# Moving the opening's sums of squares and modulation tiles between engines

## The chip, the cores and the metric

The kernel runs on one core of a Trainium2 chip. The metric is device time in microseconds (us), the median of several executions. The engines of a core work from queues of their own: TensorE (PE, with its weight loads shown apart as PEld), VectorE (DVE), ScalarE (ACT), GpSimd (POOL), and SyncE (SP), which here issues nearly all DMA transfers.

## The reference

One inference step of a one-layer hybrid trunk, over 512 prompt tokens and 32 sample tokens at once (544 columns), with 1024 features. What matters here is the beginning:

```
mod = silu(c) @ w_ada + b_ada        # shift1, scale1, gate1, shift2, scale2, gate2
h   = rms_norm(x, g_norm1) * (1 + scale1) + shift1
q, k, v, B, C, u, g_a, g_b = split(h @ w_in)
```

`c` has two rows, one of the prompt and one of the sample, so each of the six modulations is 1024 features by 2. Behind it come stick-breaking attention of 16 heads, a short gated convolution, two branch products, an output product, a second norm and a convolutional FFN, all of which the change leaves alone.

## The kernel before, in words

Activations lie feature by token: 8 feature tiles of 128 partitions, 544 columns each, in two halves of 272. A product in nearly full precision is made of three products of rounded parts: each operand is split in a high part `h` and a low part `l` (ACT casts the high part, DVE or POOL subtracts for the low one), and TensorE sums high by high, high by low and low by high. One output tile is a loop over the 8 feature tiles of the input, called a step each, with 3 x 2 = 6 matmuls of 272 columns in a step (`mm3_steps`, L112), 48 in a product.

The opening, up to the first attention scores, is this:

- Eight transfers bring `xt`, one brings `c` to all partitions (`cbc`). ACT squares each tile (L289), DVE adds the squares (`sacc1`, L291), and two fp32 matmuls with a matrix of ones (L294) give the sums over features in every partition. `rstd_of` makes the inverse root `y1` of them: Ln and Exp on ACT (L171, L173), four operations on DVE (L172 to L177).
- `mod(s, k, on_pe)` makes one of the 16 tiles of scale1 and shift1: a transfer of 512 KB into one of seven buffers `mraw` (L305), then one of two ways. On DVE, `dot` (L197) multiplies the tile by each row of silu(c) and sums, two passes over 1024 columns. On TensorE (L309) silu(c) (`sct`, 128 x 2) is the stationary operand and the tile of weights the moving one, eight fp32 matmuls of 128 columns; an fp32 matmul stands in the trace as two records, so a tile has 16. The 2 x 128 result is copied by ACT (`rc`, L312) and transposed by TensorE (L314). ACT then adds the bias and writes `mods` (L319, L321).
- Ten tiles go to DVE (all scale1, and shift1 of k = 5 and 6), six to TensorE.
- For each k, `xt` is multiplied by `y1` (L331, on POOL for four of the eight, on DVE for the others), ACT applies scale and shift (L333), and the result is split in `hh` and `hl` (L91 and L92).
- Four weight tiles of `w_in` are loaded and split meanwhile (`load_w`, L99 on ACT and L100 on POOL): for queries 0, keys 0, values 0 and queries 1.
- In program order the products of queries 0 and keys 0 (in the PSUM tiles called `slot`) come after all that, then `fill(13)`: the eight steps of values 0 and five of queries 1. `queries` and `keys` (L233 to L248) turn the results into operands for the scores `z` (L362). The `slot` tiles must be read before `z` may take their PSUM.

The order is not that of the source: a planner goes through the program and puts each engine's instructions in a fixed order by priority (earlier in the program first) and by when its own cost model thinks that their inputs are there. On the chip each engine then works strictly in this order and waits where an input is late. [...]

Of the kernel before, what the change touches and what calls it, by code (L numbers as in the profile page):

```python
# [12 lines left out]
F32 = mybir.dt.float32  # L13
F32R = mybir.dt.float32r
AF = mybir.ActivationFunctionType
ALU = mybir.AluOpType
# [18 lines left out]
# Token columns of every [feature, token] tile, as two halves, the latest token first:  # L35
# prompt 511..256 | sample 31..16, prompt 255..0 | sample 15..0.
# [4 lines left out]
# Columns of the per-partition vectors that are packed into one array.  # L41
# [9 lines left out]
def build(tc, a):  # L51
    nc = tc.nc
    ctx = ExitStack()
    with ctx:
# [4 lines left out]
        # ---------------------------------------------------------------- constants  # L59
# [16 lines left out]
        # ---------------------------------------------------------------- helpers  # L76
        def two(t):
            """A [p, T] view as its two halves."""
            return t.rearrange("p (a c) -> p a c", a=2)

        def parts(t):
            """Prompt columns and sample columns of a [p, 2, HT] view."""
            return t[:, :, 0:HP], t[:, :, HP:HT]

        def inorder(t):
            """Prompt and sample columns, as halves, of a [p, T] view with all prompt columns first."""
            return two(t[:, 0:SEQ]), two(t[:, SEQ:T])

        def split(hi, lo, x, eng=nc.vector):
            """hi + lo == x, each with 12 significant bits."""  # L90
            nc.scalar.copy(hi, x)  # L91
            eng.tensor_tensor(lo, x, hi.bitcast(F32), ALU.subtract)  # L92
# [32 lines left out]
        def proj(w, x):  # L125
            """Product with a weight tile, in DRAM or loaded."""
            if not isinstance(w, tuple):
                w = load_w(w)
            ps = acc()
            mm3(ps, *w, *x)  # L130
            return ps

        def steps(src, post, lo):
            """The product of x with a weight tile in steps, and what follows it."""
            w = src if isinstance(src, tuple) else load_w(src, lo=lo)
            ps = acc()
            yield from mm3_steps(ps, *w, *x)
            post(ps)
# [6 lines left out]
        def fill(n):  # L145
            """n steps of the products that wait in the queue."""
            while n and queue:
                try:
                    next(queue[0])
                    n -= 1  # L150
                except StopIteration:
                    queue.popleft()

        def after(inst, earlier):
            """Order two instructions of one engine."""
            tc.add_manual_dep(inst.ins, earlier.ins.name,
                              mybir.DependencyInfo(mybir.DependencyClass.NoSync, mybir.DependencyReason.DATA))

        def log_tables(earlier):
            """Load the table set that has Ln and Exp, after an activation that needs another one."""  # L160
            t = nc.scalar.add_instruction(mybir.InstLoadActFuncSet(
                name=nc.get_next_instruction_name(), act_func_set_id=6, engine=mybir.EngineType.Activation,
                ins=[], outs=[]))
            after(t, earlier)
            return t

        def rstd_of(pool, ss_ps, y, tables):
            """y = (mean + eps) ** -0.5 of the column sums in psum, in every partition."""
# [5 lines left out]
            # one Newton step: y * (1.5 - 0.5 v y y)  # L174
# [9 lines left out]
        # ---------------------------------------------------------------- adaLN  # L184
# [9 lines left out]
        def dot(raw, sums):  # L194
            """Each row of raw times silu(c), summed."""
# [4 lines left out]
        def ada(s, t):  # L200
            """mods[:, s, t, :]: one feature tile of one of the last four modulations, both batches."""
# [9 lines left out]
        # ---------------------------------------------------------------- first norm, first projections  # L211
# [6 lines left out]
        def flat(ps, name):  # L218
            """psum to [p, T] with all prompt columns first."""
# [9 lines left out]
        def queries(j, ps):  # L229
            """A head's (hi, lo) over each other, hi on the head's own partitions."""  # L230
# [7 lines left out]
        def keys(j, ps):  # L238
            """A head's (hi, hi) and (lo, lo)."""
# [16 lines left out]
        def values_t(j):  # L256
            """[keys, quarters]: head 0 hi, lo; head 1 lo, hi."""
# [11 lines left out]
        # sample queries, keys and values of all heads, kept until all are there  # L269
# [14 lines left out]
        nc.sync.dma_start(cbc, a["c"].rearrange("(o n) d -> o n d", o=1).broadcast_to([P, 2, D]))  # L284
        silu = nc.scalar.activation(cbc, cbc, AF.Silu)
        sacc1 = stp.tile([P, T], F32, name="sacc1")
        for k in range(KD):
            sq = sacc1 if k == 0 else stp.tile([P, T], F32, tag="sq", bufs=3, name="sq")
            nc.scalar.activation(sq, xt[:, k], AF.Square)  # L289
            if k:  # L290
                nc.vector.tensor_tensor(sacc1, sacc1, sq, ALU.add)  # L291
        ss = slots[0][:, :, 0:HT]
        for i in range(2):
            nc.tensor.matmul(ss[:, i], ones, two(sacc1)[:, i], start=True, stop=True)  # L294
# [7 lines left out]
        def mod(s, k, on_pe):  # L302
            """mods[:, s, k, :]: one feature tile of one of the first two modulations."""
            raw = stp.tile([P, D], F32, tag="araw", bufs=7, name="mraw")
            nc.sync.dma_start(raw, a["w_shift"][k] if on_pe else a["w_ada"][s * KD + k])  # L305
            if on_pe:
                rows = mt[0:2, 0, k % 4 * P:k % 4 * P + P]
                for i in range(KD):
                    nc.tensor.matmul(rows, sct[:, i], raw[:, i * P:i * P + P], start=i == 0, stop=i == KD - 1,  # L309
                                     skip_group_check=True)  # L310
                rc = stp.tile([2, P], F32, tag="rc", bufs=2, name="rc")
                nc.scalar.copy(rc, rows)  # L312
                sums = mt[:, 1, 2 * k:2 * k + 2]
                nc.tensor.transpose(sums, rc, ident[0:2, 0:2])  # L314
# [8 lines left out]
        ws = []  # L323
        for k in range(KD):
            if k in (1, 2, 4, 5):
                src = (W[0], W[KD], W[2 * KD], W[1])[len(ws)]
                ws.append(load_w(src, pool=stp if len(ws) < 2 else wp, lo=nc.gpsimd))
            mod(1, k, False)
            mod(0, k, k not in (5, 6))
            hf = xt[:, k]  # L330
            (nc.gpsimd if k in (1, 2, 4, 6) else nc.vector).tensor_tensor(hf, hf, y1, ALU.mult)  # L331
            for n, v in enumerate(parts(two(hf))):
                nc.scalar.activation(v, v, AF.Identity, scale=mods[:, 1, k, n:n + 1], bias=mods[:, 0, k, n:n + 1])  # L333
            split(hh[:, k], hl[:, k], hf, nc.gpsimd if k in (4, 5) else nc.vector)
        for w, slot, post in zip(ws, slots, (queries, keys)):
            ps = slot[:, :, 0:HT]
            mm3(ps, *w, *x)
            post(0, ps)
        task(values, 0, ws[2])
        task(queries, 1, ws[3])  # L340
        fill(13)
# [3 lines left out]
        # ---------------------------------------------------------------- projections and prompt attention  # L345
# [18 lines left out]
        def causal(t, width, fill):  # L364
            """Fill where the key is not before the query: [queries, blocks of width keys], last key first."""
# [4 lines left out]
        def scores(j, e):  # L370
            """One head's weights for the prompt: queries on partitions, keys from the last one back."""
# [27 lines left out]
        def transposed(sg):  # L399
            """The weights with keys on partitions, split, by rows of key blocks."""  # L400
# [15 lines left out]
        def weighted(j, e, rows, vt):  # L416
            """Weights times values, into the pair's features."""
# [17 lines left out]
        # ---------------------------------------------------------------- short conv: B * dwconv(C * u)  # L435
        def padded(t):
            """Prompt and sample columns, as halves, of a row of two stretches with two pads after each."""
# [10 lines left out]
        def conv(c, u, w, b, i):  # L448
            """Three causal taps over u's two padded stretches, latest token first."""
# [63 lines left out]
        # ---------------------------------------------------------------- sample attention, half of the heads  # L513
        def sample_steps(p0):
            """Heads of the pairs p0..p0+3: four heads' queries on the partitions, two such groups."""
# [55 lines left out]
            # the shares of the weights' high and low parts, then of the values' high and low parts  # L571
# [33 lines left out]
        # ---------------------------------------------------------------- branches and merge  # L605
# [32 lines left out]
        # ---------------------------------------------------------------- out projection, residual, second norm  # L638
# [8 lines left out]
        def streams(c0, c1):  # L647
            """The stretches of prompt and of sample columns in c0..c1, of one half."""
# [3 lines left out]
        def residual(ps, s, m, c0, c1):  # L652
            """xr[m] += gate * psum in the columns c0..c1; its squares into sacc, the last ones into sq2."""
# [11 lines left out]
        def norm(c0, c1, tables, parts_):  # L665
            """The rstd of the columns c0..c1."""
# [8 lines left out]
        def h2(c0, c1, earlier=None):  # L675
            """The second norm's output in the columns c0..c1."""
# [45 lines left out]
        # ---------------------------------------------------------------- conv FFN  # L722
# [30 lines left out]
        # the last tile's weights stay, so that one half's norm runs beside the other half's product  # L753
# [88 lines left out]
```

## Time and profile before

| | us |
|---|---|
| median of 3 runs | 1123.7 (1121.96 to 1124.98) |
| profiled execution, first to last instruction (span) | 1122.7 |
| profiled execution, whole time | not listed; the span stands 1.0 below the median |
| PE busy | 1053.6 (94%) |
| PEld busy | 1027.6 (92%) |
| DVE busy | 666.1 (59%) |
| ACT busy | 428.6 (38%) |
| POOL busy | 262.4 (23%) |
| first score matmul `z` starts | 72.78 |

Busy times are unions over an engine's instructions. The end of a matmul in the records is modelled, so spacings between starts say more than durations. [...] A stretch before the first recorded change of the clock is shown as 1.00.

### The profile page before, as it was taken

How to read it: one execution, taken by the hardware profiler on the slowest of the kernel's cores; microseconds unless marked ns; L12 is line 12 of the kernel's file. 1: busy time of each engine (PE TensorE's matmuls, PEld its weight loads, DVE VectorE, ACT ScalarE, POOL GpSimd, SP SyncE). 2: the span in 40 equal slices, each digit the busy share in tenths (PEclk: the TensorE clock that was granted, in tenths of full speed). 3: DMA queues.
4: the chain of work that ended last, by engine and by line, in shares of the span. 5: the costliest groups of instructions: out<-in, count | busy, mean ns of one | idle time of the engine just before them, and what ended most of it. 6: DMA issues, size and time to landing. Idle time of an engine off the chain costs nothing.

```text
span 1122.7 us, 19599 instructions
## 1 busy us (share of the span) xinstructions
PE 1053.6 (94%) x8042; PEld 1027.6 (92%) x8042; DVE 666.1 (59%) x1005; ACT 428.6 (38%) x749; POOL 262.4 (23%) x384
## 2 busy tenths in 40 slices
PE   3898888898999999999999999899999999999995
PEld 1688787887999999999999999899999999999995
DVE  6967787776775534666677756755455455422334
ACT  5466566565643322222222253333333333322230
POOL 3434455443321101211211215300010010001112
PEclk9899999999999999999999999899999999999998
DMA  9612121211122222455455463022222222222212
GB/s 372 217 40 95 58 78 50 73 61 67 68 88 73 79 73 94 152 187 175 165 182 178 167 228 115 1 74 78 95 91 79 95 93 77 87 90 85 85 53 80
DMA packets 38153, 120.60 MB, mean 107 GB/s; under 512 B 4272, under 2 KB 7472, under 8 KB 37936
## 3 DMA queue, kind: packets, MB, share of 16 engines
q1 hardware_dynamic: 37920, 119.22, 30.9%
q8 instruction: 63, 1.03, 0.4%
q10 hardware_dynamic: 144, 0.14, 0.1%
q14 instruction: 26, 0.21, 0.1%
HBM read 112.60 MB, written 6.75 MB: 106 GB/s over the span
## 4 chain that ended last, share of the span: by engine, by line
PE 79%; DVE 10%; ACT 4%; issue 3%; POOL 2%; DMA 1%; DVEq 0%; SPq 0%; ACTq 0%; POOLq 0%
PE ps L112 72%; DVE keep L392 3%; PE o L362 2%; PE at L408 1%; POOL keep L367 1%; DVE hf L682 1%; DVE sg L393 1%; ACT keep L388 1%; DVE adum L197 1%; PE slot L112 1%; DVE kt L246 1%; DMA cbc<-in_c_dram 1%; ACT wh L99 1%; PE so L362 1%; ACT sg L389 1%
## 5 line engine op out<-in xcount | busy, mean ns | idle before, releaser
L99 ACT CAST wh<-raw 128x1024 fp32r<-128x1024 f32 x153 | 159.7, 1045 | 349.0 <-PE ps L112 246.0
L100 DVE TENSOR_TENSOR wl<-raw,wh 128x1024 fp32r<-128x1024 f32 (+1 forms) x120 | 146.4, 1222 | 169.6 <-ACT wh L99 169.0
L112 PE MATMUL ps<-hh,wh 128*128 128x272 f32 x992 | 212.0, 295 | 8.1 <-ACT qs L235 8.1
L112 PE MATMUL ps<-hl,wh 128*128 128x272 f32 x992 | 206.8, 290 | 0.0
L112 PE MATMUL ps<-hh,wl 128*128 128x272 f32 x992 | 206.6, 290 | 0.0
L112 PEld LDWEIGHTS ps<-hh,wh 128*128 128x128 f32 x992 | 157.9, 191 | 11.0 <-ACT qs L235 9.6
L112 PEld LDWEIGHTS ps<-hl,wh 128*128 128x128 f32 x992 | 157.8, 191 | 0.0
L112 PEld LDWEIGHTS ps<-hh,wl 128*128 128x128 f32 x992 | 156.9, 191 | 0.0
L112 PE MATMUL ps<-h2l,wh 128*128 128x272 f32 x704 | 150.6, 290 | 0.9 <-DVE h2l L92 0.9
L112 PE MATMUL ps<-h2h,wh 128*128 128x272 f32 x704 | 150.9, 290 | 0.3 <-ACT h2h L91 0.3
L112 PE MATMUL ps<-h2h,wl 128*128 128x272 f32 x704 | 151.1, 291 | 0.0
L100 POOL TENSOR_TENSOR wl<-raw,wh 128x1024 fp32r<-128x1024 f32 x33 | 81.9, 2481 | 203.9 <-ACT wh L99 194.3
L112 PEld LDWEIGHTS ps<-h2l,wh 128*128 128x128 f32 x704 | 113.4, 190 | 1.7 <-DVE h2l L92 1.7
L112 PEld LDWEIGHTS ps<-h2h,wh 128*128 128x128 f32 x704 | 113.6, 190 | 0.9 <-ACT h2h L91 0.8
L112 PEld LDWEIGHTS ps<-h2h,wl 128*128 128x128 f32 x704 | 112.6, 190 | 0.0
L197 DVE SCALAR_TENSOR_TENSOR adum<-araw,cbc 128x1024 f32<-128x1024 f32 x64 | 82.7, 1293 | 41.8 <-DMA araw<-in_w_ada_dram 41.0
L392 DVE TENSOR_TENSOR_SCAN keep<-keep,zero 128x512 f32<-128x512 f32 (+1 forms) x64 | 65.9, 1041 | 8.1 <-POOL keep L367 6.3
L112 PE MATMUL ps<-fl,wh 128*128 128x272 f32 x308 | 63.9, 288 | 0.0
L367 POOL TENSOR_SCALAR_AFFINE_SELECT keep<-keep 128x128 f32<-128x128 f32 x64 | 44.3, 693 | 83.5 <-issue 43.7
L112 PE MATMUL ps<-fh,wh 128*128 128x272 f32 x308 | 63.6, 288 | 0.0
L112 PE MATMUL ps<-fh,wl 128*128 128x272 f32 x308 | 63.5, 288 | 0.0
L662 POOL TENSOR_TENSOR sacc<-sacc,sq 128x272 f32<-128x272 f32 x24 | 27.5, 1162 | 143.3 <-ACT sq L660 143.3
(200 smaller groups left out, 1745.6 us busy)
## 6 DMA issues: line engine op xcount, KB each, us to landing
raw<-in_w_in_dram SPq DMA_DIRECT2D x64, 512.0 KB, 3.3
raw<-in_w_up_dram SPq DMA_DIRECT2D x44, 512.0 KB, 3.3
araw<-in_w_ada_dram SPq DMA_DIRECT2D x32, 512.0 KB, 4.0
raw<-in_w_down_dram SPq DMA_DIRECT2D x16, 512.0 KB, 3.5
mraw<-in_w_ada_dram SPq DMA_DIRECT2D x10, 512.0 KB, 7.3
raw<-in_w_branch_b_dram SPq DMA_DIRECT2D x8, 512.0 KB, 3.2
raw<-in_w_branch_a_dram SPq DMA_DIRECT2D x8, 512.0 KB, 3.3
raw<-in_w_out_dram SPq DMA_DIRECT2D x8, 512.0 KB, 3.8
```

The source lines that it names most:

```text
L99: nc.scalar.copy(wh[:, :nk], raw[:, :nk])
L100: lo.tensor_tensor(wl[:, :nk], raw[:, :nk], wh[:, :nk].bitcast(F32), ALU.subtract)
L112: nc.tensor.matmul(ps[:, i, 0:c1 - c0], w[:, k], x[:, k0 + k, c0:c1], start=s, stop=e)
L197: nc.vector.scalar_tensor_tensor(adum, raw, 1.0, cbc[:, n], ALU.mult, ALU.mult, accum_out=sums[:, n:n + 1])
L246: nc.vector.tensor_tensor(kt[s, e, 1], kf[s], kt[s, e, 0].bitcast(F32), ALU.subtract)
L362: nc.tensor.matmul(out, l, r, start=s, stop=t, skip_group_check=True)
L367: nc.gpsimd.affine_select(out=t, in_=t, pattern=pat, compare_op=ALU.is_gt, fill=fill, base=0, channel_multiplier=-1)
L388: nc.scalar.activation(kb, z[:, c:c + w], AF.Sigmoid, scale=-(HD ** -0.5))
L389: nc.scalar.activation(sb, z[:, c:c + w], AF.Sigmoid, scale=HD ** -0.5)
L392: nc.vector.tensor_tensor_scan(kb, kb, zero.broadcast_to([P, w]), 1.0, ALU.mult, ALU.add)
L393: nc.vector.tensor_tensor(sb, sb, kp[:, s0:s0 + w], ALU.mult)
L662: nc.gpsimd.tensor_tensor(sacc[:, c0:c1], sacc[:, c0:c1], sq, ALU.add)
```

## The change

The squares are no longer added on DVE: for each k, two fp32 matmuls with ones add the square's columns into the PSUM sums. ACT's silu of `cbc` is ordered behind the last square. `mod` on TensorE has its operands exchanged: each 128 x 128 block of the weight tile is stationary and the two columns of silu(c) are moving, so the result is at once 128 x 2 in `mt`, without copy and transpose. Scale1 for even k and all of shift1 go this way (12 tiles), scale1 for odd k stays on DVE (4 tiles). The array `w_shift` becomes `w_mod`, with the tiles of both modulations. All multiplications by `y1`, and the low parts of the four weight tiles and of `h`, go to DVE. The first three products are written into the loop over k: at k = 2 three steps of each, then one step of each per k. The rest of the diff takes away comments.

```diff
         nc.sync.dma_start(cbc, a["c"].rearrange("(o n) d -> o n d", o=1).broadcast_to([P, 2, D]))
+        ss = slots[0][:, :, 0:HT]
+        for k in range(KD):
+            sq = stp.tile([P, T], F32, tag="sq", bufs=3, name="sq")
+            last = nc.scalar.activation(sq, xt[:, k], AF.Square)
+            for i in range(2):
+                nc.tensor.matmul(ss[:, i], ones, two(sq)[:, i], start=k == 0, stop=k == KD - 1)
         silu = nc.scalar.activation(cbc, cbc, AF.Silu)
-        sacc1 = stp.tile([P, T], F32, name="sacc1")
-        for k in range(KD):
-            sq = sacc1 if k == 0 else stp.tile([P, T], F32, tag="sq", bufs=3, name="sq")
-            nc.scalar.activation(sq, xt[:, k], AF.Square)
-            if k:
-                nc.vector.tensor_tensor(sacc1, sacc1, sq, ALU.add)
-        ss = slots[0][:, :, 0:HT]
-        for i in range(2):
-            nc.tensor.matmul(ss[:, i], ones, two(sacc1)[:, i], start=True, stop=True)
+        after(silu, last)
...
-            nc.sync.dma_start(raw, a["w_shift"][k] if on_pe else a["w_ada"][s * KD + k])
+            nc.sync.dma_start(raw, a["w_mod"][s * KD + k] if on_pe else a["w_ada"][s * KD + k])
             if on_pe:
-                rows = mt[0:2, 0, k % 4 * P:k % 4 * P + P]
+                sums = mt[:, s, 2 * k:2 * k + 2]
                 for i in range(KD):
-                    nc.tensor.matmul(rows, sct[:, i], raw[:, i * P:i * P + P], start=i == 0, stop=i == KD - 1,
+                    nc.tensor.matmul(sums, raw[:, i * P:i * P + P], sct[:, i], start=i == 0, stop=i == KD - 1,
                                      skip_group_check=True)
-                rc = stp.tile([2, P], F32, tag="rc", bufs=2, name="rc")
-                nc.scalar.copy(rc, rows)
-                sums = mt[:, 1, 2 * k:2 * k + 2]
-                nc.tensor.transpose(sums, rc, ident[0:2, 0:2])
...
-        ws = []
+        ws, products = [], []
         for k in range(KD):
-            if k in (1, 2, 4, 5):
-                src = (W[0], W[KD], W[2 * KD], W[1])[len(ws)]
-                ws.append(load_w(src, pool=stp if len(ws) < 2 else wp, lo=nc.gpsimd))
-            mod(1, k, False)
-            mod(0, k, k not in (5, 6))
+            mod(1, k, k % 2 == 0)
+            mod(0, k, True)
+            if k < 4:
+                ws.append(load_w((W[0], W[KD], W[2 * KD], W[1])[k], pool=stp if k < 2 else wp))
+            if k == 2:
+                products = [mm3_steps(slot[:, :, 0:HT], *w, *x) for w, slot in zip(ws, slots)]
+                products.append(steps(ws[2], lambda ps: values(0, ps), None))
             hf = xt[:, k]
-            (nc.gpsimd if k in (1, 2, 4, 6) else nc.vector).tensor_tensor(hf, hf, y1, ALU.mult)
+            nc.vector.tensor_tensor(hf, hf, y1, ALU.mult)
...
-            split(hh[:, k], hl[:, k], hf, nc.gpsimd if k in (4, 5) else nc.vector)
-        for w, slot, post in zip(ws, slots, (queries, keys)):
-            ps = slot[:, :, 0:HT]
-            mm3(ps, *w, *x)
-            post(0, ps)
-        task(values, 0, ws[2])
+            split(hh[:, k], hl[:, k], hf)
+            for g in products:
+                for _ in range(3 if k == 2 else 1):
+                    next(g)
+        for slot, post in zip(slots, (queries, keys)):
+            post(0, slot[:, :, 0:HT])
+        for _ in products[2]:
+            pass
         task(queries, 1, ws[3])
-        fill(13)
+        fill(5)
```

## Rows read from the trace of the kernel before

**Rows 1.** The page: busy time by engine, and PE in 40 slices of the span.
```profile
PE 1053.6 (94%) x8042; PEld 1027.6 (92%) x8042; DVE 666.1 (59%) x1005; ACT 428.6 (38%) x749; POOL 262.4 (23%) x384
...
PE   3898888898999999999999999899999999999995
```

**Rows 2.** Stretches of 80 us: PE, PEld, DVE, ACT, POOL busy, PEclk, DMA, GB/s.
```profile
0.00:80.00 80.00, 55.38 (x336) 43.66 (x337) 60.71 (x74) 46.17 (x87) 29.13 (x36) 0.94 0.58 221
...
400.00:480.00 80.00, 80.00 (x640) 79.98 (x639) 44.40 (x69) 21.60 (x27) 10.64 (x16) 1.00 0.34 113
```

**Rows 3.** Waits, 0 to 80 us: who for whom, us in total, times, longest.
```profile
ACT mods L319 <- DVE adum L197: 9.3, 4, 4.5
...
PE mt L309 <- ACT mods L321: 0.4, 1, 0.4
```

**Rows 4.** Waits of the DMA issuing queue SP, 0 to 80 us.
```profile
SPq L305 <- DVE adum L197: 16.1, 5, 5.0
```

**Rows 5.** Groups by line and shape, 0 to 80 us: busy, mean ns, idle before.
```profile
L197 DVE SCALAR_TENSOR_TENSOR adum<-mraw,cbc 128x1024 f32<-128x1024 f32 x20 | 34.0, 1702 | 3.0 <-ACT cbc L285 2.5
...
L92 DVE TENSOR_TENSOR hl<-xt,hh 128x544 fp32r<-128x544 f32 x6 | 4.3, 720 | 3.5 <-ACT hh L91 3.5
```

**Rows 6.** The opening in order of time: start us, us, engine, line.
```profile
4.29 0.66 ACT L289 ACTIVATE sacc<-xt 128x544 f32<-128x544 f32 x1
...
12.61 1.91 ACT L285 ACTIVATE cbc<-cbc 128x2048 f32<-128x2048 f32 x1 [1.76 <-DMA cbc<-in_c_dram]
...
15.82 1.22 DVE L197 SCALAR_TENSOR_TENSOR adum<-mraw,cbc 128x1024 f32<-128x1024 f32 x1
...
18.53 2.75 POOL L100 TENSOR_TENSOR wl<-raw,wh 128x1024 fp32r<-128x1024 f32 x1 [16.98 <-ACT wh L99]
...
19.00 3.37 DVE L197 SCALAR_TENSOR_TENSOR adum<-mraw,cbc 128x1024 f32<-128x1024 f32 x1
...
22.30 0.71 DVE L177 SCALAR_TENSOR_TENSOR y<-nt,y 128x544 f32<-128x544 f32 x1
...
68.33 0.60 ACT L233 CAST qt<-slot 64x544 fp32r<-64x544 f32 x1 [1.98 <-PE slot L112]
...
72.78 1.49 PE L362 MATMUL z<-kt,qt 128*128 128x512 f32 x8 [0.47 <-ACT qs L235]
```

**Rows 7.** TensorE in order of time: sums, modulation tiles, products, a later norm.
```profile
12.21 2.15 PE L294 MATMUL slot<-sacc,ones 128*128 128x272 f32 x4 [12.21 <-DVE sacc L291]
...
19.80 3.58 PE L309 MATMUL mt<-mraw,sct 128*2 128x128 f32 x16 [0.35 <-ACT mods L321]
...
45.09 1.91 PE L309 MATMUL mt<-mraw,sct 128*2 128x128 f32 x16
...
690.60 0.68 PE L669 MATMUL ssh<-sq,ones 128*128 128x272 f32 x2
691.12 0.62 PE L669 MATMUL ssh<-sacc,ones 128*128 128x272 f32 x2
```

**Rows 8.** Weight loads of 128 columns before short matmuls, in order of time.
```profile
103.53 0.19 PEld L362 LDWEIGHTS o<-al,vt 128*128 128x128 f32 x1
...
103.64 0.19 PEld L362 LDWEIGHTS o<-ah,vt 128*128 128x128 f32 x1
...
355.48 0.18 PEld L362 LDWEIGHTS so<-sa,vo 32*128 32x128 f32 x1
355.71 0.19 PEld L362 LDWEIGHTS so<-sa,vc 128*128 128x128 f32 x1
```

**Rows 9.** Stretches of 5 us in the opening, columns as in rows 2.
```profile
20.00:25.00 5.00, 3.37 (x16) 1.77 (x14) 5.00 (x6) 0.81 (x2) 3.19 (x2) 1.00 1.03 420
...
30.00:35.00 5.00, 1.79 (x12) 0.98 (x10) 5.00 (x4) 0.25 (x1) 3.95 (x2) 0.94 0.30 118
35.00:40.00 5.00, 4.78 (x20) 3.67 (x21) 4.97 (x10) 3.53 (x7) 0.20 (x1) 0.50 0.32 108
40.00:45.00 5.00, 5.00 (x34) 4.03 (x32) 4.53 (x4) 1.84 (x6) 2.20 (x1) 0.88 0.64 206
```

More of the change, by code (lines that the diff above doesn't have):

```diff
@@ L807 @@
         "vec": np.concatenate(vec, axis=1),
-        "w_shift": tiles(i["w_ada"][0, :, :D]).reshape(KD, P, D),
+        "w_mod": tiles(i["w_ada"][0, :, :2 * D]).reshape(2 * KD, P, D),
         "w_ada": i["w_ada"][0].T.reshape(6 * KD, P, D),
```

## The prediction

> **What bounds the kernel now.** I read the page first. TensorE is busy 94% of the span, and its slices show where it is not: the first [rows 1]. Next the stretches of 80 us. The first has 55.4 us of PE in 80; from 400 on PE is full, 640 matmuls in 80 us, so a 272-column matmul costs 80/640 = 0.125 us once nothing is late [rows 2]. Only a loose stretch can give time, and the change edits one only: all up to the first score matmul `z` at 72.78. Behind it the same work is left in the same order, with the same thirteen steps of values 0 and queries 1 already done, so I carry a shift of `z` one to one to the end. That is the frame of every number below.
>
> Then who waits in the opening. ACT waits for sums from DVE, 9.3 us in four waits for scale1 alone [rows 3]; the loads wait 16.1 us for DVE to free a buffer [rows 4]. DVE spends 34.0 us on 20 passes of `dot`, mean 1.70 [rows 5], though a pass beside no POOL work takes 1.22; one that overlaps POOL's subtraction (18.53 to 21.28) takes 3.37 [rows 6]. So DVE, slowed beside POOL, sets the pace before; transfers ran at 420 GB/s in 20 to 25 and at 118 and 108 in 30 to 40 [rows 9].
>
> **DVE after.** Eight passes at 1.22 are 9.8 us in place of 34.0. The low parts cost more there: eight of `h` at 0.72 [rows 5], two more than before, and four weight tiles of 1024 columns, which I take at 1.22 like a pass of the same width: 4.9. The eight multiplications by `y1` have the columns of an `hl` and go at 0.72: 5.8. The rest of the norm is four operations at 0.71 [rows 6]: 2.9. In all 9.8 + 5.8 + 4.9 + 5.8 + 2.9 = 29.2 us between about 13 and the end of the opening, with no POOL operation beside it: DVE no longer sets the pace. If slowing is not POOL's doing, the eight passes cost 13.6 instead, and DVE is still under TensorE's sum below.
>
> **Loads.** The 512 KB tiles are as many as before, 16 and 4. At 420 GB/s one takes 1.25 us. `cbc` lands before 12.61, when its silu starts [rows 6], so the last of 20 lands at about 12.6 + 25 = 37.6. SP issues them in a row unless a buffer is held; TensorE can hold them now, but then TensorE is the pace.
>
> **TensorE after: the sum.** It starts with the first square at 4.29 + 0.66 = 4.95 [rows 6].
>
> Sums of squares: 16 matmuls, 32 records. The old four took 2.15 us, 0.5 each with the modelled end taken off, and two pairs of a later norm start 0.52 apart, 0.26 each [rows 7]. [...] From 35 the records show a granted 0.50 and, in 40 to 45, 0.88, that is 1.2 us more at half: 6 us of work before it rose, after the loose stretch 30 to 35 [rows 9]. So 6 us at 0.5 are 12 records and 20 at 0.26 are 5.2: 11.2 us, to 16.2. Ends: 32 x 0.26 = 8.3 and 32 x 0.5 = 16. The old sum was done by 14.4, but `y` got its last operation only at 22.30, behind passes of `dot` [rows 6]. Now Ln, Exp and three operations follow in about 4 us: `y1` stands at 20 to 21. The silu behind the squares costs nothing, because `cbc` lands after them anyway; if squares wait for the sums through three buffers, it moves with them, which the same 4 us allow.
>
> Twelve modulation tiles: 16 records each, a 128-column fp32 load with two moving columns, a form that the trace lacks. Bounds: loads before short matmuls start 0.11 apart in one place and 0.23 in another [rows 8]: 16 x 0.11 = 1.76 and 16 x 0.23 = 3.7 us. The old tile took 1.91 between dense products and 3.58 after a loose stretch [rows 7], 0.12 and 0.22 a record. I take 1.91, nearest to the row with full 128-partition loads in a row: 22.9 us. At 3.58 it is 43.0.
>
> [...]
>
> Products: 3 x 48 + 30 matmuls up to `z`, as before; 174 x 0.125 = 21.8 us.
>
> Hand-overs: a tile's matmuls write a bank of `mt` that ACT has to have read. Before, one such wait was 0.4 us [rows 3] and another 0.35 [rows 7]. Twelve at 0.4: 4.8. If the planner puts a product's step into each, they cost 0; if ACT is in the middle of its 2.4 us per feature, up to 2 each. The removed copy and transpose are off this path.
>
> Sum: 4.95 + 11.2 + 22.9 + 21.8 + 4.8 = 65.7 for the work ahead of `z`, against 72.8: 7.1 us earlier. The work on queries and keys after their last matmul (68.33 to 72.78 before [rows 6]) has 3.75 us of queries 1 beside it as it had, and I leave it inside the sum. The span becomes 1122.7 - 7.1 = 1115.6, and with the 1.0 between span and median 1116.6. What is late next is TensorE itself: its work ahead of `z` fills the time from 5 to `z`.
>
> The same sum gives the turning point: without the tiles it is 42.8, and (72.8 - 42.8)/12 = 2.5 us. The change pays if a tile costs TensorE less than 2.5 us, and this lies between the bounds.
>
> **The rivals.**
> A, slower: the tiles run at the lower clock. They are on TensorE from about 16, ahead of the first dense steps, and between waits. For it: the tile at 19.80 took 3.58, and the clock stood at 0.50 after a stretch with PE busy 1.79 us in 5 [rows 7, 9]. Against: three products mix in from about 25. With half of the tiles at 3.58, TensorE's sum is 75.7 and the time 1126.6; with all, 85.8 and 1136.7. The middle is 1131. [...]
>
> B, slower: each load waits for the short matmul before it, 0.23 us a record. 3.7 us a tile, sum 87, time 1138 at the full clock. For it the `so` pair, against it the `o` pair [rows 8].
>
> C, much faster: a tile at 1.3 us or less and hand-overs hidden. 4.95 + 11.2 + 15.6 + 21.8 = 53.6, 19 us earlier, 1104.5. It cannot go far beyond: the last tile lands at 37.6, and dot, bias, scale, split (about 5.3), three last steps (2.3) and the 4.4 to `z` end at 50. For it: no row shows a load alone. Against: close loads are 0.11 apart.
>
> D, no gain: the fixed order. The planner believes its own times; where TensorE arrives at a tile before its load or its bank, everything behind stands. Seven us of such waits eat the 7.1: 1123.7, give or take 3.
>
> **How the numbers follow.** Forecast 0.43, A 0.25, B 0.10, C 0.07, D 0.15. Predicted 1116.6. The forecast's own range is 1112 to 1120 (hand-overs 0 to 8 us). With C and most of A the range is 1105 to 1134. A measurement of this kernel can tell about 0.3%, 3.4 us: faster means under 1120.3, slower over 1127.1. Faster: 0.43 + 0.07 + 0.04 of D = 0.54. Same: 0.11 of D + 0.02 of A = 0.13. Slower: 0.33.
>
> **What would show it.** Right: `z` starts near 66; the sums' 32 records end near 16; a tile's 16 records take about 1.9 us; DVE passes are all near 1.22 with POOL idle; PE is busy from 5 to `z` in nearly every stretch of 5 us. A shows as a granted 0.50 over the tiles and records 0.22 apart, B as records 0.23 apart at 1.00. C shows as PE idle and DMA at its 420 GB/s until 37. D shows as waits of PE on `mods` or on loads of many us. The prediction is wrong if `z` comes early and the end does not, that is if the attention stretch gives the time back.

## The result

The changed kernel is slower: 1132.9 us (1125.9 to 1133.5) against 1122.8 for the kernel before, ratio 1.007 (95% interval 1.005 to 1.009). The forecast was 1116.6, faster. The profiled execution has a span of 1130.8, 8.1 more than before; `z` starts at 84.36 in place of 72.78, 11.6 later. A row or a `z` is of the one profiled execution, a time is the median of all; the executions of one kernel lie up to 8 us apart, the longer ones mostly at the lower mean granted clock (in one kernel 1124.0 at 0.971 and 1132.2 at 0.962).

The page after: busy time by engine, PE and granted clock (PEclk, as a share of TensorE's full rate) in 40 slices.
```profile
PE 1074.8 (95%) x8160; PEld 1057.2 (93%) x8160; DVE 642.5 (57%) x984; ACT 425.5 (38%) x743; POOL 239.0 (21%) x374
...
PE   7988898888899999999999999899999999999995
...
PEclk8688999999999999999999999999999999999998
```
Against [rows 1], PE is fuller in the opening, and the clock row shows why that did not help. Stretches of 80 us (columns as in [rows 2]):
```profile
0.00:80.00 80.00, 71.03 (x385) 67.97 (x386) 29.65 (x47) 35.13 (x63) 1.84 (x19) 0.74 0.56 210
```
PE 71 us in place of 55, DVE 30 in place of 61, clock 0.74 in place of 0.94. Stretches of 5 us, against [rows 9]:
```profile
15.00:20.00 5.00, 4.56 (x31) 4.39 (x29) 2.17 (x3) 3.15 (x5) 0.00 (x0) 0.79 1.02 408
20.00:25.00 5.00, 4.65 (x22) 4.51 (x21) 2.62 (x3) 1.19 (x2) 0.00 (x0) 0.50 1.03 412
25.00:30.00 5.00, 4.65 (x23) 4.61 (x22) 5.00 (x9) 4.04 (x9) 0.00 (x0) 0.50 1.03 409
30.00:35.00 5.00, 5.00 (x24) 5.00 (x24) 2.56 (x5) 2.27 (x6) 0.00 (x0) 0.50 0.58 182
...
40.00:45.00 5.00, 4.65 (x41) 4.56 (x40) 2.13 (x4) 0.54 (x2) 0.00 (x0) 1.00 0.08 11
45.00:50.00 5.00, 4.56 (x23) 4.47 (x24) 0.00 (x0) 1.36 (x3) 0.00 (x0) 0.52 0.94 349
```
TensorE is busy over 90% of each. Yet in 20 to 35 it is granted 0.50, and 0.52 in 45 to 50: before, the 0.50 of 35 to 40 stood behind a stretch with PE busy 1.79 us in 5 [rows 9], here the clock falls while tiles run with waits of at most 0.44 us between them. It falls at or right behind two-column tiles (in 15 to 20, 45 to 50, 60 to 65 and 70 to 75, granted 0.79, 0.52, 0.73 and 0.75) and rises in runs of products (in 35 to 40, 55 to 60, 65 to 70 and 75 to 80, granted 0.66, 0.96, 0.59 and 0.91). TensorE in order of time, against [rows 7] and the last line of [rows 6]:
```profile
15.40 1.84 PE L307 MATMUL mt<-sct,mraw 128*128 128x2 f32 x16
17.69 3.42 PE L307 MATMUL mt<-sct,mraw 128*128 128x2 f32 x16 [0.44 <-ACT mods L313]
21.46 3.58 PE L307 MATMUL mt<-sct,mraw 128*128 128x2 f32 x16 [0.35 <-ACT mods L315]
...
34.20 0.66 PE L112 MATMUL slot<-hl,wh 128*128 128x272 f32 x2
34.65 0.65 PE L112 MATMUL slot<-hh,wh 128*128 128x272 f32 x2
...
44.05 2.56 PE L307 MATMUL mt<-sct,mraw 128*128 128x2 f32 x16 [0.35 <-ACT mods L315]
47.05 3.57 PE L307 MATMUL mt<-sct,mraw 128*128 128x2 f32 x16 [0.44 <-ACT mods L313]
...
84.36 1.48 PE L360 MATMUL z<-kt,qt 128*128 128x512 f32 x8 [2.48 <-ACT qs L235]
```
Of the twelve tiles five take 1.84 to 1.95 us, one 2.56 and six 3.41 to 3.58. The products among them slow down too: at a granted 0.50 two matmuls start 0.45 us after the two before them, where 2 x 0.125 is 0.25. DVE's passes, against [rows 5], are what was forecast:
```profile
L197 DVE SCALAR_TENSOR_TENSOR adum<-mraw,cbc 128x1024 f32<-128x1024 f32 x8 | 9.8, 1221 | 0.0
```

### The profile page after: what moved, and what is told of

It reads as the page before. It is cut to its first block, busy times and chain, and to the rows that moved or that the text cites. A ratio compares the mean times of both kernels' runs of the same rounds, so it can differ in the third digit from the quotient of the medians.

```text
span 1130.8 us, 19780 instructions
## 1 busy us (share of the span) xinstructions
PE 1074.8 (95%) x8160; PEld 1057.2 (93%) x8160; DVE 642.5 (57%) x984; ACT 425.5 (38%) x743; POOL 239.0 (21%) x374
## 4 chain that ended last, share of the span: by engine, by line
PE 82%; DVE 10%; ACT 4%; POOL 2%; issue 2%; DMA 0%; DVEq 0%; ACTq 0%; POOLq 0%
PE ps L112 72%; DVE keep L390 3%; PE mt L307 3%; PE o L360 2%; PE slot L112 2%; DVE hf L680 1%; PE at L406 1%; POOL keep L365 1%; DVE sg L391 1%; DVE kt L246 1%; ACT keep L386 1%; PE slot L290 1%; PE so L360 1%; DVE qt L234 1%; DVE kt L244 1%
## 5 line engine op out<-in xcount | busy, mean ns | idle before, releaser
L100 DVE TENSOR_TENSOR wl<-raw,wh 128x1024 fp32r<-128x1024 f32 (+1 forms) x124 | 151.3, 1222 | 170.4 <-ACT wh L99 169.8
L100 POOL TENSOR_TENSOR wl<-raw,wh 128x1024 fp32r<-128x1024 f32 x29 | 70.1, 2419 | 176.7 <-ACT wh L99 176.7
L390 DVE TENSOR_TENSOR_SCAN keep<-keep,zero 128x512 f32<-128x512 f32 (+1 forms) x64 | 68.2, 1075 | 7.8 <-POOL keep L365 6.0
```

Of the source, the lines that this page charges most:

```text
L100: lo.tensor_tensor(wl[:, :nk], raw[:, :nk], wh[:, :nk].bitcast(F32), ALU.subtract)
L390: nc.vector.tensor_tensor_scan(kb, kb, zero.broadcast_to([P, w]), 1.0, ALU.mult, ALU.add)
```

## The experiments

Times below are medians; the kernel before measured 1121.9 to 1123.3 beside them.

**112 moving columns.** The tiles and their number stay; the moving operand grows, and eight DVE copies ahead of them make it. The edit, shortened:
```
-  nc.tensor.matmul(sums, raw[:, i*P:i*P+P], sct[:, i], ...)
+  nc.tensor.matmul(wide, raw[:, i*P:i*P+P], sctw[:, i] (56 copies of the two columns), ...)
+  sums = wide[:, 0:2]
```


> The changed kernel, but each tile's matmuls on TensorE stream 112 columns (56 copies of the two of silu(c), made by eight small DVE copies) past the same stationary weights instead of 2; only the first two results are used. Clock theory (the tiles with two moving columns let TensorE fall to its lower clock, and tiles and products then run at half rate): the granted clock stays at 1.00 over most of the opening, a tile's 16 records take about 1.9 us in place of a mean of 2.75, z starts at 66 to 70 in place of 84.4, and the time falls from about 1133 to 1116 to 1122. Work theory (twelve tiles and 32 sum records are simply too much for TensorE, at any clock): more columns can only add, z at 84 or later, 1133 or more. Order theory (the products written into the loop make TensorE wait): nothing changes, 1133 give or take 3.

1121.7 us, ratio to before 0.998 (0.997 to 1.000), 11 below the changed kernel. More columns for TensorE to stream, and in the profiled execution an opening 15 us shorter. Its stretches and tiles:
```profile
25.00:30.00 5.00, 4.84 (x37) 4.55 (x38) 5.00 (x8) 3.19 (x7) 0.00 (x0) 1.00 1.03 410
...
45.00:50.00 5.00, 4.87 (x40) 4.83 (x40) 1.34 (x4) 4.04 (x9) 0.00 (x0) 1.00 1.02 383
```
```profile
17.40 2.04 PE L310 MATMUL mt<-sctw,mraw 128*128 128x112 f32 x16 [0.44 <-ACT mods L317]
...
69.45 1.49 PE L364 MATMUL z<-kt,qt 128*128 128x512 f32 x8 [2.00 <-ACT qs L235]
```
Both are shown at 1.00, as is every stretch up to 80, so the rate of the records has to tell: 37 and 40 in the two where the changed kernel has 23 in each, and a tile at 1.93 to 2.04. The work theory falls; the clock theory holds to the number of `z` (66 to 70). The order theory expected no change. The planner's order did shift with the wide operand (two tiles are split by steps of products), and how much of the 15 us this gives is open; but a record every 0.22 us within one tile (3.58 at a granted 0.50, changed kernel) and every 0.12 here (1.93) is not a matter of order.

The profiled execution took 1118.0 at a mean granted clock of 0.983, and only one of the nine others was like it. Eight took 1121.5 to 1123.5 at 0.973 to 0.977, so in them the clock was down for longer; where, no trace shows.

**The old operand form for twelve tiles.** On TensorE silu(c) is stationary again and 128 weight columns are moving, with copy and transpose; the rest is as changed.


> The changed kernel with the operands of the twelve TensorE tiles as they were before: silu(c) stationary, 128 columns of weights moving, then the copy by ACT and the transpose; all else as changed. Clock theory: the clock holds as in the kernel with 112 columns, the copy and transpose add some 0.5 us of hand-over each, z at 68 to 74, time 1118 to 1126. Work theory: at least as much work, 1133 or more. Order theory: 1133 give or take 3.

1123.6, `z` at 75.38. The clock holds here as well (every tile 1.91, shown at 1.00), and each tile pays for its copy and transpose:
```profile
19.17 1.91 PE L307 MATMUL mt<-mraw,sct 128*2 128x128 f32 x16 [0.44 <-ACT mods L317]
21.42 0.22 PE L312 MATMUL mt<-ident,rc 2*128 2x2 f32 x1 [0.35 <-ACT rc L310]
```
`z` is 5.9 us later than with 112 columns on stationary weights, 0.49 a tile, though the medians lie only 1.8 apart. So exchanging the operands does save what it removes, and with two columns, at a granted 0.50 over half of the tiles, it loses more: `z` at 84.36, 9.0 later than here.

**Eight tiles on TensorE, two columns.** The edit is `mod(1, k, False)`: all of scale1 on DVE.


> The changed kernel with all eight scale1 tiles on DVE, so eight instead of twelve on TensorE, two moving columns as changed. Clock theory: the clock still falls in the opening, but four tiles of 2.75 us less are on TensorE (-11 us); DVE gets eight passes of 1.22 more (+10 on an engine with 45 us to spare): z at 72 to 76, time 1121 to 1126. Work theory: the same -11 us without a change of the clock; the two are told apart by the other runs. Order theory: 1133 give or take 3.

1120.7, `z` at 73.01. As the clock theory had it, 0.3 under its time: four tiles fewer, and three of the eight still take 3.41 to 3.57, a fourth 3.4 in two parts, the others 1.84 to 1.95. The work theory would allow this run as well.

**Eight tiles, 112 columns.** Both edits.


> Eight tiles on TensorE and 112 moving columns together. Clock theory: clock up and four tiles fewer, TensorE's sum is 4.95 + 10.6 + 8 x 1.9 + 21.8 + 3.2 = 55.8; with a dot chain of DVE at its end z at 58 to 64, time 1108 to 1115, faster than both kernels. Work theory: as with eight tiles of two columns, 1121 to 1126. Order theory: 1133 give or take 3.

1113.4, ratio 0.991 (0.990 to 0.993), `z` at 65.5 (1.5 later than hoped): faster than both kernels. The clock does not hold throughout:
```profile
25.55 3.54 PE L310 MATMUL mt<-sctw,mraw 128*128 128x112 f32 x16
```
This tile runs behind a stretch, 20 to 25, with PE busy 1.40 us in 5, and 25 to 30 is granted 0.66. So 112 columns do not keep the clock behind every idle stretch (with twelve tiles it held behind one of 1.83 in 5). TensorE also waits 2.5 us ahead of `z`, as in the changed kernel.

**Eight tiles in the old form.**


> The changed kernel with eight tiles on TensorE in the form of before (silu(c) stationary, 128 moving weight columns, copy and transpose), all scale1 tiles on DVE. Clock theory: the clock holds as with 112 columns, and only the copies and transposes (about 0.5 us each on the way of a tile) are added: z at 66 to 70, time 1113 to 1118, several us below the eight stationary tiles with two moving columns (1120.7). If stationary weights were the gain by themselves: 1120 or more.

1122.6, a miss: no better than eight stationary tiles of two columns. The clock did not hold as the theory wanted: the tiles at 18.70 and 25.24 take 3.45 and 3.55, behind waits of 1.70 us for `rc` and 2.04 for `hh`, though 128 columns are moving. `z` at 69.65 is in the range, 4.2 behind eight tiles of 112 columns. Some 1.5 of that is one more slow tile (3.45 against 1.91); the rest would be 0.3 a tile for copy and transpose, which no run parts further. The profiled execution took 1120.9, the second shortest of ten (1118.6 to 1123.6); why the median lies 9 us above that of eight tiles of 112 columns, with `z` only 4.2 later, stays open.

**The sums back on DVE.** The added lines of the diff's first part undone.


> The changed kernel with the squares added on DVE as before, so four sum records on TensorE instead of 32, all else changed. Clock theory: the sums are the work that brings the clock up once before the tiles; without them the tiles begin at the lower clock at about 14.5, TensorE has 8 us less to do but the work was ahead of the first tile's load in any case; z at 82 to 87, time 1130 to 1136. Work theory: 8 us less work of TensorE gives z at 76 and about 1125.

1133.3, `z` at 86.27. TensorE has 8 us less work and nothing is gained: the first tile starts at 14.70 in place of 15.40 and takes 3.41 in place of 1.84. On the median the sums on TensorE cost nothing net; the trace is of the longest of the four executions (1137.6).

**The kernel before, with the operand exchange alone.** Six tiles, two columns.


> The kernel before with one edit: its six TensorE tiles take the weights as stationary operand and two moving columns, without copy and transpose. There DVE sets the pace, and TensorE is idle for about 25 us ahead of z. Clock theory: tiles at the lower clock take 3.5 us each in place of a mean of 3.07, in time that TensorE has, and the products between them run more often at the lower clock: z within 72 to 78, 1122 to 1128. If the exchange were bad or good by itself (loads not hidden, or copies saved): bad 1130 or more, good 1119 or less.

1127.6, ratio 1.005 (1.003 to 1.006): this one edit makes the old kernel slower. Five of its six tiles take 3.41 to 3.58 us (before, two took 3.57 and 3.58, three 2.93 to 3.22, one 1.91), and the products ahead of `z` keep PE busy for 32.0 us in place of 27.2. `z` is at 80.0, 2 beyond the expected range, in the longest of the ten executions (1130.3).

**One low part from POOL to DVE, in the changed kernel.**
```
-  task(keys, j + 1, W[KD + j + 1], nc.gpsimd)
+  task(keys, j + 1, W[KD + j + 1], nc.gpsimd if j else nc.vector)
```


> The changed kernel with one instruction moved from POOL to DVE, the low part of the weights of keys 1; the orders of TensorE, ACT and SP stay the same. Collision theory: DVE's two low parts of keys 0 take 1.45 us in place of 3.60 and z starts about 2 us earlier, near 82; the clock still falls with the tiles: 1129 to 1132 against 1132.9, still slower than before. If the collision were the cause of the whole loss: 1123 or less.

1129.2 (1124.0 to 1132.2), ratio 1.005 to before. DVE ahead of `z`, in the changed kernel and then in this one:
```profile
79.73 3.60 DVE L246 TENSOR_TENSOR kt<-kf,kt 64x544 fp32r<-64x544 f32 x2
```
```profile
78.59 1.47 DVE L246 TENSOR_TENSOR kt<-kf,kt 64x544 fp32r<-64x544 f32 x2
```
The same two instructions, beside POOL's subtraction (79.61 to 82.00) and not beside it. `z` starts 4.8 us after ACT's first read of `slot`, not 7.0. Beside 2.4 us of POOL they take 2.1 us longer; by what the two engines hold each other up no row shows.

**The same in the kernel with eight tiles and 112 columns.**


> Eight tiles on TensorE, 112 moving columns, and one instruction moved from POOL to DVE: the low part of the first weight tile that the attention stretch loads (keys 1), which on POOL lay beside DVE's low parts of keys 0 (two of 0.72 us took 3.60 together, and z waited). Collision theory: those two go back to about 1.45 us, z starts 2.0 to 2.5 us earlier than the 65.5 with it on POOL, and the time falls from 1113.4 to about 1111. If the hand-over to z is bound by ACT instead: z unchanged within 0.5, 1113 to 1114.

1110.6, ratio 0.989 (0.988 to 0.991): the fastest kernel of the study, 22 us below the changed one. `z` at 63.89, 1.6 earlier. TensorE's wait ahead of `z` shrinks by 2.1, from 2.47 to 0.35; a second slow tile (3.34 at 19.22, where it took 2.01; 20 to 25 is granted 0.50) takes part of it back.

**Six tiles, 112 columns.** Two shift tiles more on DVE.


> The kernel with eight tiles of 112 columns and keys 1's low part on DVE (1110.6), with two more shift tiles (k = 3 and 6) on DVE: six on TensorE, ten on DVE, as many as before. If TensorE still sets the pace: two tiles of 2.0 us less, z 3 to 4 us earlier than 63.9, 1107 to 1109. If DVE sets it now (four passes of 1.22 more): z the same or later, 1110 to 1114.

1113.9, ratio 0.992 (0.990 to 0.994): no better than with eight, and probably slower, as the intervals of the two ratios overlap a little. TensorE now waits 5.9 us for `hh` (three waits) and `z` is at 64.6. Of six, eight and twelve tiles, eight came out best.

## Why the prediction was wrong

The frame was right: the end moves with `z`, nearly. From `z` to the end it is 1049.9 us before, 1046.4 after, and between 1044.6 and 1049.5 in the ten other kernels; what makes these 5 us is open, and the 3.5 that the changed kernel gets back lie there. One of its four executions took 1125.9, at a mean granted clock of 0.968 where the other three have 0.963 to 0.965; why its clock was up for longer is open too.

DVE's part was right: passes at 1.22, POOL idle from 5 to 75, and the terms of the sum stand in the trace as 9.8, 5.8, 4.9, 5.6 and 2.9 us, 29.0 against 29.2. TensorE did become the pace, busy from 5 on.

The sums were right: 10.56 us against 11.2. No run shows that the 0.5 and 0.26 a record in that term are the rates of a lower and an upper clock, as all of the sums are shown at 1.00; what the trace has is 11 of the records in 5 to 10 and 21 in 10 to 15, 0.45 and 0.24 us each.

The tiles failed, the step "I take 1.91". At a granted 1.00 (41.85) a tile does take 1.84, a record every 0.115 us, so the bound of 0.23 (rival B) is out; and 110 more moving columns add at most 0.013 us to a record (2.04 a tile), where a product's matmul of 272 costs 0.125. But the twelve took 33.0 us, not 22.9, because the clock was at 0.50 for half of them. This is what rival A said, at the price of its half case.

The products failed with them, and rival A had not counted that: "174 x 0.125 = 21.8" was taken from a stretch at a granted 1.00. PE was busy 30.6 us with the 174 matmuls, against 24.9 with 112 columns (shown at 1.00) and 27.2 before: some 5.7 us are the clock's, and 3.1 were missing from the term at any clock. Tiles and products came out 10.1 and 8.8 us above their terms, 18.9 together, and `z` 18.7 later than the sum's 65.7. The mean tile, 2.75, is past the turning point of 2.5; by the sum this alone makes `z` 3 us later than before, and the other 8.6 of the 11.6 are about what the products cost above their term. That rival A's middle, 1131, is close to 1132.9 is luck: it stands for more slow tiles, not for slow products.

The hand-overs were right, and somewhat cheaper than priced: seven waits of tiles for ACT, 2.7 us in sum, against twelve and 4.8. What is waited for is not only ACT's read of the same half of `mt`: the shift1 tile at 17.69 waits 0.44 us for the read of a scale1 tile, which lies in the other half. With one of a product (0.4) and one for `hh` (0.9) PE waited 4.0 for ACT in the tile stretch (columns: us in sum, count, longest):
```profile
PE mt L307 <- ACT mods L315: 1.4, 4, 0.4
PE mt L307 <- ACT mods L313: 1.3, 3, 0.4
```
Not foreseen: TensorE's wait of 2.5 us ahead of `z` (0.5 before), 2.1 of it by the POOL collision.

What I misread was [rows 9]. I took the idle time before 35 as what lowers the clock, and so, in the forecast, a TensorE without gaps for one at the upper clock. The old tile had 128 moving columns, the new one two; the trace before had no row of the new form, and I priced its duration from both sides but not its effect on the clock, for the tiles and for what runs behind them. Rival A put the tiles between waits and had a tile behind a loose stretch for it; here the fall came in stretches with 90 to 93% of PE busy and no wait of a tile above 0.44 us.

## What to carry to other kernels

Read the granted clock beside the busy share: in 20 to 35 here TensorE, with two-column tiles for most of it, counted as busy for 4.65 to 5.00 us in 5 and was granted 0.50, and the products behind the tiles started in pairs 0.45 us apart in place of 0.25. Before an edit makes the moving operand narrow, ask what keeps the clock up; with twelve tiles here, copies of the columns did (2.0 us a tile at 112 columns, 1.84 at two, 3.6 at two with the clock at 0.50). With eight tiles, behind a stretch with PE busy 1.40 us in 5, one still took 3.54. Where two engines share the load of an opening, try the split again once the clock holds.

## What was unexpected in the hardware

More columns, less time: widening the moving operand from 2 to 112 columns added 0.1 to 0.2 us to a tile that was not slowed (1.84 to 1.93 and 2.04) and took 11 us off the kernel. And the form with 128 moving columns kept the clock in the changed kernel all through the tiles (1.91 each of the twelve), while the same form in the kernel before ran in a stretch at 0.50 from 35 on (3.22 at 38.50), behind one with PE busy 1.79 us in 5, and with eight tiles two of them took 3.45 and 3.55.
